# Pairs of keys apart, and VectorE squares for softmax sums and new rows

## The chip, the cores and the metric

The kernel runs on one core of a Trainium2 chip. The metric is the device time of one execution in microseconds (us). A core has TensorE (PE in the profile, its weight loads PEld), VectorE (DVE), ScalarE (ACT), GpSimd (POOL) and SyncE (SP), which here issues every transfer (DMA). Each engine works through its own queue in order.

## The reference

One layer of an encoder with two head groups, for a prompt of 1024 rows and a sample of 32 rows, all in float32:

- `hn = rmsnorm(h)`; `[qA kA vA gA qB kB vB gB] = hn @ w_in`, each 512 wide: 8 heads of 64.
- A: band attention. Scores `q k / 8` plus a position bias, softmax over a frame's own chunk of 64 and the 8 chunks before it.
- B: stick-breaking attention, strictly causal: weight = sigmoid(z) times the product of sigmoid(-z) over the keys between.
- `y = concat(oA * silu(gA), oB * silu(gB)) @ w_out`; `h = h + rmsnorm(y)`; `h = h + sigmoid(h @ w_ple_gate) * (p @ w_ple)`.

Outputs are the two results and the new keys and values of A and B, of the prompt (A: the last 512 rows; B: all) and of the sample (32 rows).

## The kernel before, in words

The 1056 rows (`T`: 1024 of the prompt, `SEQ`, and 32 of the sample) are normed and turned once, then projected in three chunks of 352 columns. A projected group `st` has features on partitions and rows in columns; columns 1024 to 1055 are the sample's. Heads are worked in pairs, A0 B0 A1 B1 A2 B2 A3 B3; while one pair's attention runs, the next pair's k, q, v are projected, and the gates `gA`, `gB` at the end (`weave` puts the two streams together). After that come the output product and the gate product.

Attention takes a head's queries in blocks of 128, i = 0 to 7. For each block there are three steps: scores (`scores`), turning of the weights, so that keys lie on partitions (`weights_t`), and, once per four blocks, the product with the values (`values`). In A a block has `cost(i)` = i + 1 key blocks, at most 5; in B i + 1. In `scores`, A takes score plus bias and the running extreme on VectorE (into `om`), then ScalarE makes the exponential (`om` to `be`) and its sum into a column of `sums`. In B ScalarE makes sigmoids, VectorE a running product (`TENSOR_TENSOR_SCAN`), and GpSimd a difference (`om` to `be`).

The weights are turned in one of two ways. Blocks 0 to 3 (and B's last, 7) go through TensorE: transposes into the PSUM banks with tag "T" (two of them; tiles `ptwA`, `ptwB`), from which ScalarE and VectorE take a rounded part `wTh` and the rest `wTl`. Blocks in `ROUND` (A: 4 to 7, B: 4 to 6) are turned by squares of 32 by 32 on VectorE (`STREAM_TRANSPOSE`, `om` from `be`), go out to a DRAM scratch (`swapA`, `swapB`) and come back with the four partition groups in place (`be` from `swapA`), and are then split into `wTh` and `wTl`. For this the four columns of a group of four keys have to lie apart, in four stretches. The view `apart` does it when the exponential or the difference is written:

```
return x.rearrange("p (b c k) -> p b k c" if out else "p (b k c) -> p b k c", c=4, k=32)
```

Consecutive elements are so written 32 columns (128 bytes) from one another, and the transpose reads its input in a row.

Three small things are also turned on TensorE, each by one transpose into a "T" bank and a ScalarE copy: A's softmax sums (`ptsA`, evicted to `sumrowA`, [8, 128], stored to `rs_dr`, from which the gates read them over partitions as `oggA`), the sample's 32 new rows of keys (`ptkA`, `ptkB`, in `short_block`, called by `keys_out`) and of values (`ptvA`, `ptvB`, by `values_out`). The sums are preceded by a reciprocal on VectorE. The long part of keys is turned by squares (`ktA`, `ktB`) and stored by quarters of partitions. The long part of values is turned by squares that read every second column (`vxA`, `vxB`), goes through a scratch and back into `st`, and is copied to `vtA`, `vtB`, from which `prep_v` makes `v2A`, `v2B`. The new rows of values are stored twice, to the output and to the scratch `vs_dr`, from which the sample's attention loads them. The tiles `kt`, `vx`, `vt` share the tag "tok" (two buffers).

Nothing is issued in the order in which it is written. A recorder notes every operation with what it depends on; a planner with fixed prices per operation (`cost`) plays the program through, gives each operation off TensorE a due time (`due`), and fixes every engine's order (`plan`), four times over. TensorE's priorities are the order of recording. The price of a transpose on VectorE is 100 + 1.04 ns per column, or another for a view with four axes. All instructions stand under line 497 in the profile, where the recorder emits them; they are told apart by the names of their tiles.

Of the kernel before, what the change touches and what calls it, by code (L numbers as in the profile page):

```python
# [8 lines left out]
F32 = mybir.dt.float32  # L9
# [4 lines left out]
P = 128  # L14
D = 1024
SEQ = 1024
NS = 32
T = SEQ + NS
# [484 lines left out]
def stream_step(  # L503
# [20 lines left out]
        return Buf(shape, F32, name=name, real=dram.tile(shape, F32, tag=name, name=name))  # L524

    o_dr = [scratch([P, T], f"o_dr{n}") for n in range(8)]
    rs_dr = scratch([8, T], "rs_dr")
    og_dr = scratch([8, P, T], "og_dr")
    h1_dr = scratch([T, D], "h1_dr")
    sum_dr = {w: scratch([4, 4, P, 512], f"sum_dr{w}") for w in "og"}  # L530
# [41 lines left out]


    NAMES = ["qA", "kA", "vA", "gA", "qB", "kB", "vB", "gB"]

    def fixed_columns():
        x = small.tile([8, NS], F32, tag="fixed", name="fixed")
        nc.gpsimd.memset(x, 1.0)
        dma(rs_dr[:, SEQ:T], x)

    raws, loaded = {}, {}

# [48 lines left out]

    def scale_x(t, xt, n, gp):
        sq = ring1.tile([P, D], f"sq{t}")
        ms = small.tile([P, 1], F32, tag="ms", name=f"ms{t}", bufs=4)
        nc.scalar.activation(sq[0:n], xt[0:n], AF.Square, scale=1.0 / 32.0, accum_out=ms[0:n])
        r = rstd_of(ms, f"rs{t}", n)
        for kh in range(2):
            nc.vector.scalar_tensor_tensor(sq[0:n, HALF[kh]], xt[0:n, HALF[kh]], r[0:n], gp[kh][0:n], ALU.mult, ALU.mult)
        return sq
# [65 lines left out]
        return (0 if ab == "A" else 4) + p  # L705


    def short_block(src, out, nm):
        pt = psum("T", nm)
        nc.tensor.transpose(pt[0:NS, 0:P], src[:, SEQ:T], ident)  # L710
        nc.scalar.copy(out[0:NS, 8, :], pt[0:NS, 0:P])

    def keys_out(ab, p, src, o_p, o_s):

        n = SEQ // 2 if ab == "A" else SEQ
        h2 = slice(2 * p, 2 * p + 2)

        def turn():
            out = at2.tile([P, NT, P], F32, tag="tok", name=f"kt{ab}{p}", bufs=2)
            x = out.rearrange("p b c -> p (b c)")[:, 0:n]  # L720
            nc.vector.transpose(x, src()[:, SEQ - n:SEQ])
            rows = o_p[0, 0, :, h2, :].rearrange("(c t) h d -> t c (h d)", t=32)
            for g in range(4):
                q = slice(32 * g, 32 * g + 32)
                dma(rows[:, :, q], x[q].rearrange("t (c f) -> t c f", f=32))
            short_block(src(), out, f"ptk{ab}{p}")
            dma(o_s[0, 0, :, h2, :].rearrange("p h d -> p (h d)"), out[0:NS, 8, :])

        return [(0.1, turn)]

    def values_out(ab, p, src, o_p, o_s, then):

        h2 = slice(2 * p, 2 * p + 2)
        b0 = 4 if ab == "A" else 0
        box = {}

        def turn():
            st = src()
            D = scratch([2, 4, HD, SEQ // 4], f"swap{ab}{p}")
            x = at2.tile([P, SEQ], F32, tag="tok", name=f"vx{ab}{p}", bufs=2)  # L740
            nc.vector.transpose(x.rearrange("p (i j b f) -> p b i j f", i=2, j=2, f=32), st[:, 0:SEQ].rearrange("p (b i t j) -> p b i j t", i=2, t=32, j=2))
            dma(D.rearrange("i g (t j) x -> (g t) i (j x)", j=2), x.rearrange("p (i x) -> p i x", i=2))
            for i in range(2):
                dma(st[HD * i:HD * i + HD, 0:SEQ].rearrange("p (g x) -> p g x", g=4), D[i].rearrange("g p x -> p g x"))
            out = at2.tile([P, NT, P], F32, tag="tok", name=f"vt{ab}{p}", bufs=2)
            box["out"] = out
            short_block(st, out, f"ptv{ab}{p}")

        def back():
            out = box["out"]  # L750
            nc.scalar.copy(out[:, 0:8, :].rearrange("p b (g f) -> p g b f", g=4), src()[:, 0:SEQ].rearrange("p (g b f) -> p g b f", g=4, f=32))
            dma(o_p[0, 0, :, h2, :].rearrange("(b p) h d -> p b (h d)", p=P), out[:, b0:8, :])
            dma(o_s[0, 0, :, h2, :].rearrange("p h d -> p (h d)"), out[0:NS, 8, :])
            then(out)

        return [(0.1, turn), (0.0, back)]
# [7 lines left out]
    def col_steps(j):  # L764
# [56 lines left out]

        def after_v(tok):
            src_of["v", ab, p] = tok
            dma(vs_dr[ab][:, p * P:(p + 1) * P], tok[0:NS, 8, :])

        if k == "q":
            steps.append((0.0, after_q))
# [8 lines left out]
    def attention(ab, p, h):  # L836
# [5 lines left out]
        def begin():  # L842
            if ab == "A":
                bias = at2.tile([P, 640], F32, tag="bias", name=f"bias{nm}", bufs=2)
                dma(bias, bias_src(2 * p + h, P, 0, 640))
                nc.gpsimd.memset(bias[0:HD, 0:HD], -NEG)
                nc.gpsimd.memset(bias[HD:P, 576:640], -NEG)
                box["bias"] = bias
                box["sums"] = small.tile([P, 8], F32, tag="sums", name=f"sums{nm}", bufs=2)

        def lo_block(i):
            return max(0, i - 4) if ab == "A" else 0
# [19 lines left out]
        def apart(i, x, out=False):  # L872

            if i not in together:
                return x
            return x.rearrange("p (b c k) -> p b k c" if out else "p (b k c) -> p b k c", c=4, k=32)

        def scores(i):
            L, kd, kl = Lq[h], KDh[h], KLD[h]
            b0 = lo_block(i)  # L880
            n = (i + 1 - b0) * P
            k0 = b0 * P
            cut = [0, n] if n <= 512 else [0, n // 2, n]
            w0, w1 = rooms(i)
            pieces = []
            for j in range(len(cut) - 1):
                s = psum("S", f"S{nm}_{i}_{j}")[:, 0:cut[j + 1] - cut[j]]
                lhs = L[:, i * P:(i + 1) * P]
                ks = slice(k0 + cut[j], k0 + cut[j + 1])
                nc.tensor.matmul(s, lhs, kd[:, ks], start=True, stop=False)  # L890
                nc.tensor.matmul(s, lhs, kl[:, ks], start=False, stop=True)
                pieces.append((cut[j], cut[j + 1], s))
            if ab == "B":
                a, b, s = pieces[-1]
                dg = s[:, b - a - P:b - a]
                nc.vector.tensor_tensor(dg, dg, maskb, ALU.add)
                nc.gpsimd.memset(w0[:, n:n + 1], 1.0)
                for a, b, s in pieces:
                    nc.scalar.activation(w0[:, a:b], s, AF.Sigmoid, scale=-1.0)
                for a, b, s in reversed(pieces):  # L900
                    rev = w0[:, a:b][:, ::-1]
                    nc.vector.tensor_tensor_scan(rev, rev, s, w0[:, b:b + 1], ALU.mult, ALU.bypass)
                nc.gpsimd.tensor_tensor(apart(i, w1[:, 0:n], True), apart(i, w0[:, 1:n + 1]), apart(i, w0[:, 0:n]), ALU.subtract)
            else:
                m = small.tile([P, 4], F32, tag="stat", name=f"stat{nm}_{i}", bufs=6)
                sums = box["sums"]
                for j, (a, b, s) in enumerate(pieces):
                    nc.vector.tensor_tensor_reduce(
                        w0[:, a:b], s, box["bias"][:, n - b:n - a][:, ::-1], 1.0,
                        3e38 if j == 0 else m[:, j - 1:j], ALU.add, ALU.min, m[:, j:j + 1])  # L910
                last = len(pieces) - 1
                nc.scalar.activation(apart(i, w1[:, 0:n], True), apart(i, w0[:, 0:n]), AF.Exp, bias=m[:, last:last + 1], scale=-1.0, accum_out=sums[:, i:i + 1])
                if i == 7:
                    nc.vector.reciprocal(sums, sums)
                    pt = psum("T", f"pts{nm}")
                    nc.tensor.transpose(pt[0:8, 0:P], sums, ident)
                    row = at.tile([P, 4 * P], F32, tag="ot", name=f"sumrow{nm}", bufs=2)[0:8, 0:P]
                    nc.scalar.copy(row, pt[0:8, 0:P])
                    dma(rs_dr[2 * p + h, 0:SEQ].rearrange("(i q) -> i q", q=P), row)
            state[i] = w0, w1  # L920

        wT = {}
# [5 lines left out]
        def weights_t(i):  # L928
# [9 lines left out]
            if i in together:  # L938
# [5 lines left out]
                w0, w1 = whole[group]  # L944
                m = sum(cost(x) for x in group)
                first = {x: sum(cost(y) for y in group[:k]) for k, x in enumerate(group)}
                squares = w0[:, 0:m * P].rearrange("p (c b q) -> p b c q", c=4, q=32)
                for x, _, _ in done_with:
                    y = slice(first[x], first[x] + cost(x))
                    nc.vector.transpose(squares[:, y], w1[:, y.start * P:y.stop * P])  # L950
                dr = scratch([4, P, m * 32], f"swap{nm}_{i}")
                dma(dr.rearrange("g (k c) x -> (g k) (c x)", c=4), w0[:, 0:m * P])
                dma(w1.rearrange("p (g x) -> p g x", g=4), dr.rearrange("g p x -> p g x"))
# [493 lines left out]
        dma(*x)  # L1447
        rec.behind()
    bias_rows()
    fixed_columns()  # L1450
    for h in range(4):
        dma(masks[h * NS:(h + 1) * NS, :], maskb[0:NS, 0:NS])
    for j in range(3):
# [176 lines left out]
    class Row:  # L1630


        def __init__(self, t, h1):
            self.t, self.h1 = t, h1
            self.t0, self.n = rows_of(t)
            self.ms = small.tile([P, 2], F32, tag="ms2", name=f"ms2_{t}", bufs=4)

        def load(self):
            self.x = [wpool.tile([P, 512], F32, tag="wr", name=f"x2_{self.t}_{q}", bufs=4) for q in range(2)]
# [277 lines left out]
```

## Time and profile before

| | |
|---|---|
| median of 3 runs | 797.52 us (795.85 to 797.86) |
| the profiled execution, its own time | 796.99 us |
| span in the profile | 795.2 us |
| mean granted TensorE clock | 0.997 |
| busy: PE, DVE, ACT, POOL | 772.9, 600.3, 519.7, 447.9 us |
| moved by DMA | 177.83 MB, 224 GB/s |

The span goes from the first to the last instruction. In a row of a group stand the engine, the operation, output and input by their names in the program, the shape and the count; then the busy time, the mean in ns of one, and the engine's idle time just before them with what ended it. In a list of waits a row gives the waiting engine and tile, what it waited for, the total in us, how often, and the longest. A window's row gives its limits and length, then busy time and instructions of PE, PEld, DVE, ACT and POOL, the granted clock, the DMA engines' share, and GB/s. A timeline's row begins with the start and the duration in us. A row of transfers ends with the size of one and the median us from issue to landing. Matmuls overlap in TensorE's pipeline, and their ends are modelled.

### The profile page before, as it was taken

How to read it: one execution, taken by the hardware profiler on the slowest of the kernel's cores; microseconds unless marked ns; L12 is line 12 of the kernel's file. 1: busy time of each engine (PE TensorE's matmuls, PEld its weight loads, DVE VectorE, ACT ScalarE, POOL GpSimd, SP SyncE). 2: the span in 40 equal slices, each digit the busy share in tenths (PEclk: the TensorE clock that was granted, in tenths of full speed). 3: DMA queues.
4: the chain of work that ended last, by engine and by line, in shares of the span. 5: the costliest groups of instructions: out<-in, count | busy, mean ns of one | idle time of the engine just before them, and what ended most of it. 6: DMA issues, size and time to landing. Idle time of an engine off the chain costs nothing. (4 is left out here: it accounts for less than half of the span.)

```text
span 795.2 us, 13848 instructions
## 1 busy us (share of the span) xinstructions
PE 772.9 (97%) x4518; PEld 709.4 (89%) x4518; DVE 600.3 (75%) x1007; ACT 519.7 (65%) x1039; POOL 447.9 (56%) x503
## 2 busy tenths in 40 slices
PE   8999999999999999999999999999999999999997
PEld 6999989998999999889999888999997877888786
DVE  6716788897889985799899788985446878686655
ACT  5636686577696644896567786542349867876741
POOL 5624638883556876234652327788634358597613
PEclk9999999999999999999999999999999999999999
DMA  8519998778988869776557668884769857569734
GB/s 268 164 45 288 247 280 284 236 222 295 252 261 261 261 196 258 213 214 204 136 161 169 204 203 259 255 241 142 229 228 336 276 172 269 202 228 314 230 110 133
DMA packets 176330, 177.83 MB, mean 224 GB/s; under 512 B 38129, under 2 KB 132057, under 8 KB 176258
## 3 DMA queue, kind: packets, MB, share of 16 engines
q1 hardware_dynamic: 176258, 176.95, 73.6%
q8 instruction: 36, 0.59, 0.3%
q14 instruction: 36, 0.29, 0.1%
HBM read 107.62 MB, written 60.88 MB: 212 GB/s over the span
## 5 line engine op out<-in xcount | busy, mean ns | idle before, releaser
L497 POOL TENSOR_TENSOR be<-om 128x128 f32<-128x128 f32 (+7 forms) x64 | 84.0, 1324 | 57.2 <-DVE om L497 10.5
L497 DVE TENSOR_TENSOR_SCAN om<-om,SB 128x384 f32<-128x384 f32 (+5 forms) x96 | 94.3, 999 | 9.9 <-ACT om L497 5.0
L497 ACT ACTIVATE be<-om,statA 128x640 f32<-128x640 f32 (+4 forms) x64 | 63.9, 1021 | 9.6 <-DVE wTl L497 4.2
L497 DVE TENSOR_TENSOR wTl<-be,wTh 128x640 fp32r<-128x640 f32 (+2 forms) x56 | 62.2, 1115 | 10.6 <-ACT wTh L497 10.4
L497 DVE STREAM_TRANSPOSE om<-be 128x640 f32<-128x640 f32 (+2 forms) x56 | 49.6, 888 | 11.4 <-ACT be L497 8.0
L497 ACT ACTIVATE om<-SB 128x384 f32<-128x384 f32 (+5 forms) x96 | 44.7, 491 | 20.2 <-DVE SB L497 9.8
L497 ACT CAST wTh<-be 128x640 fp32r<-128x640 f32 (+2 forms) x56 | 43.3, 774 | 12.7 <-DMA be<-swapB 7.0
L497 POOL TENSOR_TENSOR oB<-oB,oB 128x256 f32<-128x256 f32 x32 | 26.8, 862 | 15.0 <-DMA oB<-in_w_out_dram 14.8
L497 DVE CUSTOM_DVE_ANT_0 om<-SA,biasA 128x320 f32<-128x320 f32 (+2 forms) x64 | 29.7, 482 | 7.0 <-PE SA L497 5.2
L497 POOL TENSOR_TENSOR gB<-gB,gB 128x256 f32<-128x256 f32 x32 | 28.3, 902 | 11.9 <-DMA gB<-in_w_ple_gate_dram 10.8
L497 POOL TENSOR_TENSOR klB<-stkB,kdB 64x1024 fp32r<-64x1024 f32 x8 | 19.4, 2426 | 26.7 <-ACT kdB L497 25.6
L497 PE MATMUL SB<-kdB,LB 128*128 128x384 f32 (+5 forms) x96 | 33.5, 351 | 0.7 <-DVE om L497 0.7
L497 ACT CAST wTh<-ptwB 128x512 fp32r<-128x512 f32 (+3 forms) x48 | 22.2, 482 | 17.7 <-PE ptwB L497 15.8
L497 PE MATMUL SB<-klB,LB 128*128 128x384 f32 (+5 forms) x96 | 32.9, 347 | 0.0
L497 PE MATMUL SA<-kdA,LA 128*128 128x320 f32 (+2 forms) x96 | 30.1, 323 | 0.9 <-DVE statA L497 0.7
L497 DVE TENSOR_TENSOR wTl<-ptwB,wTh 128x512 fp32r<-128x512 f32 (+3 forms) x48 | 25.2, 542 | 5.9 <-ACT wTh L497 4.5
L497 PE MATMUL SA<-klA,LA 128*128 128x320 f32 (+2 forms) x96 | 29.3, 317 | 0.2 <-DMA klA<-klA 0.2
L497 POOL TENSOR_TENSOR sggA<-sggA,oggA 128x352 f32<-128x352 f32 x24 | 25.7, 1075 | 6.4 <-DVE sggA L497 2.3
L497 POOL TENSOR_TENSOR klA<-stkA,kdA 64x1024 fp32r<-64x1024 f32 x8 | 20.9, 2608 | 6.9 <-ACT kdA L497 6.5
L497 PE MATMUL PVB<-wTh,v2B 128*128 128x512 f32 (+1 forms) x96 | 21.6, 349 | 2.8 <-DVE otA L497 1.9
L497 POOL TENSOR_TENSOR h<-h,x 128x512 f32<-128x512 f32 (+1 forms) x18 | 23.6, 1337 | 0.0
L497 POOL TENSOR_TENSOR sggB<-sggB,oggB 128x352 f32<-128x352 f32 x12 | 11.9, 988 | 20.3 <-DVE sggB L497 15.7
(707 smaller groups left out, 2630.7 us busy)
## 6 DMA issues: line engine op xcount, KB each, us to landing
swapA<-om SPq DMA_DIRECT2D x32, 320.0 KB, 4.3
be<-swapA SPq DMA_DIRECT2D x32, 320.0 KB, 4.8
oB<-in_w_out_dram SPq DMA_DIRECT2D x16, 256.0 KB, 5.2
sum_dro<-oB SPq DMA_DIRECT2D x16, 256.0 KB, 4.0
gB<-in_w_ple_gate_dram SPq DMA_DIRECT2D x16, 256.0 KB, 4.6
sum_drg<-gB SPq DMA_DIRECT2D x16, 256.0 KB, 4.7
x<-in_x_prompt_dram SPq DMA_DIRECT2D x16, 256.0 KB, 3.5
h_dr<-h SPq DMA_DIRECT2D x8, 512.0 KB, 3.9
```

What stands on the lines that cost most here:

```text
L497: getattr(getattr(tc.nc, o.what[0]), o.what[1])(*args, **kw)
```

## The change

- `apart`: of each four consecutive keys, the first two go to the first half of the block's columns and the other two to the second half, pair beside pair. Elements are so written in pairs of neighbours.
- `weights_t`: the squares read every second column of a half. Their output lies as before, and so do the transfers.
- `short_block` is gone. `keys_out` turns the sample's 32 columns in the same transpose as the long part; `values_out` does it with a transpose of its own into a wider `vx`. The new function `new_rows` stores them from 128 partitions in pieces of 32 elements, for values once to the output and once to `vs_dr`, both in `turn` (before, the row to the output was stored in `back`).
- A's sums: `sums` has 32 columns, the last 24 set to 1.0 by GpSimd at the start of a head; VectorE turns them by squares, and all 128 partitions are stored. `rs_dr` gets rows of 32 x 128; the ones that `fixed_columns` stored once for the sample's columns now come with them.
- Tags of small tiles (`ms`, `ms2`) are joined.

```diff
-    rs_dr = scratch([8, T], "rs_dr")
+    rs_dr = scratch([8, 32 * P], "rs_dr")
...
-    def fixed_columns():
-        x = small.tile([8, NS], F32, tag="fixed", name="fixed")
-        nc.gpsimd.memset(x, 1.0)
-        dma(rs_dr[:, SEQ:T], x)
...
-    def short_block(src, out, nm):
-        pt = psum("T", nm)
-        nc.tensor.transpose(pt[0:NS, 0:P], src[:, SEQ:T], ident)
-        nc.scalar.copy(out[0:NS, 8, :], pt[0:NS, 0:P])
+    def new_rows(x, dst):
+        dma(dst.rearrange("t (g f) -> g t f", f=32), x)
...
-            out = at2.tile([P, NT, P], F32, tag="tok", name=f"kt{ab}{p}", bufs=2)
-            x = out.rearrange("p b c -> p (b c)")[:, 0:n]
-            nc.vector.transpose(x, src()[:, SEQ - n:SEQ])
+            x = at2.tile([P, NT * P], F32, tag="tok", name=f"kt{ab}{p}", bufs=2)[:, 0:n + NS]
+            nc.vector.transpose(x, src()[:, SEQ - n:T])
...
-            short_block(src(), out, f"ptk{ab}{p}")
-            dma(o_s[0, 0, :, h2, :].rearrange("p h d -> p (h d)"), out[0:NS, 8, :])
+            new_rows(x[:, n:n + NS], o_s[0, 0, :, h2, :].rearrange("p h d -> p (h d)"))
...
-            x = at2.tile([P, SEQ], F32, tag="tok", name=f"vx{ab}{p}", bufs=2)
+            x = at2.tile([P, T], F32, tag="tok", name=f"vx{ab}{p}", bufs=2)
+            nc.vector.transpose(x[:, SEQ:T], st[:, SEQ:T])
+            new_rows(x[:, SEQ:T], o_s[0, 0, :, h2, :].rearrange("p h d -> p (h d)"))
+            new_rows(x[:, SEQ:T], vs_dr[ab][:, p * P:(p + 1) * P])
+            x = x[:, 0:SEQ]
...
-            short_block(st, out, f"ptv{ab}{p}")
...
-            dma(o_s[0, 0, :, h2, :].rearrange("p h d -> p (h d)"), out[0:NS, 8, :])
...
-            dma(vs_dr[ab][:, p * P:(p + 1) * P], tok[0:NS, 8, :])
...
-                box["sums"] = small.tile([P, 8], F32, tag="sums", name=f"sums{nm}", bufs=2)
+                box["sums"] = small.tile([P, 32], F32, tag="sums", name=f"sums{nm}", bufs=2)
+                nc.gpsimd.memset(box["sums"][:, 8:32], 1.0)
...
-            return x.rearrange("p (b c k) -> p b k c" if out else "p (b k c) -> p b k c", c=4, k=32)
+            return x.rearrange("p (c k d) -> p k c d" if out else "p (k c d) -> p k c d", c=2, d=2)
...
-                    nc.vector.reciprocal(sums, sums)
-                    pt = psum("T", f"pts{nm}")
-                    nc.tensor.transpose(pt[0:8, 0:P], sums, ident)
-                    row = at.tile([P, 4 * P], F32, tag="ot", name=f"sumrow{nm}", bufs=2)[0:8, 0:P]
-                    nc.scalar.copy(row, pt[0:8, 0:P])
-                    dma(rs_dr[2 * p + h, 0:SEQ].rearrange("(i q) -> i q", q=P), row)
+                    nc.vector.reciprocal(sums[:, 0:8], sums[:, 0:8])
+                    row = at.tile([P, 4 * P], F32, tag="ot", name=f"sumrow{nm}", bufs=2)[:, 0:32]
+                    nc.vector.transpose(row, sums)
+                    dma(rs_dr[2 * p + h].rearrange("(i g q) -> g i q", g=4, q=32), row)
...
-                squares = w0[:, 0:m * P].rearrange("p (c b q) -> p b c q", c=4, q=32)
+                squares = w0[:, 0:m * P].rearrange("p (i j b q) -> p i j b q", i=2, j=2, q=32)
...
-                    nc.vector.transpose(squares[:, y], w1[:, y.start * P:y.stop * P])
+                    nc.vector.transpose(squares[:, :, :, y], w1[:, y.start * P:y.stop * P].rearrange("p (i b k j) -> p i j b k", i=2, k=32, j=2))
```

More of the change, by code (lines that the diff above doesn't have):

```diff
@@ L633, in scale_x @@
         sq = ring1.tile([P, D], f"sq{t}")
-        ms = small.tile([P, 1], F32, tag="ms", name=f"ms{t}", bufs=4)
+        ms = small.tile([P, 2], F32, tag="ms", name=f"ms{t}", bufs=4)[:, 0:1]
         nc.scalar.activation(sq[0:n], xt[0:n], AF.Square, scale=1.0 / 32.0, accum_out=ms[0:n])
@@ L724, in turn @@
                 q = slice(32 * g, 32 * g + 32)
-                dma(rows[:, :, q], x[q].rearrange("t (c f) -> t c f", f=32))
-            short_block(src(), out, f"ptk{ab}{p}")
-            dma(o_s[0, 0, :, h2, :].rearrange("p h d -> p (h d)"), out[0:NS, 8, :])
+                dma(rows[:, :, q], x[q, 0:n].rearrange("t (c f) -> t c f", f=32))
+            new_rows(x[:, n:n + NS], o_s[0, 0, :, h2, :].rearrange("p h d -> p (h d)"))
         return [(0.1, turn)]
@@ L1449, in stream_step @@
     bias_rows()
-    fixed_columns()
     for h in range(4):
@@ L1635, in __init__ @@
             self.t0, self.n = rows_of(t)
-            self.ms = small.tile([P, 2], F32, tag="ms2", name=f"ms2_{t}", bufs=4)
+            self.ms = small.tile([P, 2], F32, tag="ms", name=f"ms2_{t}", bufs=4)
         def load(self):
```

## The prediction, made before the changed kernel was run

> **What bounds the kernel now.** I read the page first (busy shares), then a window over the attention stage, then what TensorE waits for, then the groups by shape.
>
> ```profile
> span 795.2 us, 13848 instructions
> PE 772.9 (97%) x4518; PEld 709.4 (89%) x4518; DVE 600.3 (75%) x1007; ACT 519.7 (65%) x1039; POOL 447.9 (56%) x503
> ```
> ```profile
> 60.00:500.00 440.00, 426.73 (x2689) 408.46 (x2688) 369.78 (x650) 311.62 (x618) 244.11 (x280) 1.00 0.81 232
> 380.00:440.00 60.00, 59.76 (x380) 57.70 (x379) 54.54 (x87) 41.69 (x80) 27.75 (x28) 1.00 0.60 162
> ```
>
> TensorE (PE) sets the time: 97% over the span. All that the change touches lies between 60 and 500 us, where the two attentions run beside the projections. There PE is busy 426.73 of 440 us, so 13.3 us of visible gaps are left, VectorE (the third busy figure) has 70.2 us free, ScalarE (the fourth) 128.4. No other engine is the bound; what can be won is a PE gap or PE work. In 380 to 440 VectorE has only 5.5 us free: it is the engine next in line.
>
> The gaps of PE, by what ended them:
>
> ```profile
> PE ptsA L497 <- DVE sumsA L497: 5.2, 7, 1.5
> PE PVB L497 <- DVE otA L497: 1.9, 1, 1.9
> PE ptkB L497 <- ACT stkB L497: 1.1, 1, 1.1
> PE PVB L497 <- ACT wTh L497: 0.9, 1, 0.9
> PE SA L497 <- DVE statA L497: 0.7, 2, 0.5
> PE SB L497 <- DVE om L497: 0.7, 2, 0.5
> PE PVA L497 <- ACT wTh L497: 0.6, 2, 0.3
> PE SsA L497 <- ACT QsA L497: 0.5, 1, 0.5
> PE ptwA L497 <- ACT sumrowA L497: 0.5, 1, 0.5
> PE ptosA L497 <- ACT be L497: 0.4, 1, 0.4
> PE ptvB L497 <- ACT stvB L497: 0.2, 1, 0.2
> ```
>
> The largest gap is a step that the change removes: PE stands still seven times for the reciprocal of A's softmax sums, to turn them (`ptsA`). The turning of new keys and values (`ptkB`, `ptvB`) and the eviction of the turned sums (`sumrowA`) add 1.1, 0.2 and 0.5. Together 7.0 us.
>
> **Part 1: the 24 small transposes leave PE.** Eight for sums, eight for new keys, eight for new values. Their own time:
>
> ```profile
> 83.96 0.27 PE L497 MATMUL ptkB<-ident,stkB 128*32 128x128 f32 x1
> 83.98 0.57 PE L497 MATMUL mm_qB<-hnh,wh_qB 128*128 128x352 f32 x2
> ```
> ```profile
> 731.08 0.87 PE pth L497 x8
> ```
>
> The matmul behind `ptkB` starts 0.02 us after it, although the row gives 0.27 for one (spans overlap in PE's pipeline); transposes in a row take 0.87/8 = 0.109 each. So 24 of them cost 0.5 us to 2.6 us; the first row is of the instruction itself, I take 0.5. With the waits, up to 7.5 us of PE. In the timeline of the first such wait, the instructions queued behind `ptsA` are score and projection matmuls, whose operands stand ready: they start at once, so what is behind the wait was held by it alone.
>
> What is late next? PE would come up to 1.5 us earlier per head to the products with the values (`PVA`), which wait for `wTh`, at the end of the chain exponential, transpose, out to DRAM and back, cast. That chain also gets shorter, by part 2: four exponentials a head. So I keep 6.0 of the 7.0, a choice, since some gaps will open elsewhere; were the exponentials not faster, half, 3.5.
>
> **Part 2: the exponential writes pairs.**
>
> ```profile
> L497 ACT ACTIVATE be<-om,statA 128x640 f32<-128x640 f32 x32 | 46.1, 1481 | 1.1 <-PE ptwA L497 1.1
> L497 ACT ACTIVATE be<-om,statA 128x512 f32<-128x512 f32 x8 | 5.8, 722 | 1.2 <-DVE wTl L497 1.1
> L497 ACT ACTIVATE be<-om,statA 128x384 f32<-128x384 f32 x8 | 4.9, 613 | 3.1 <-DVE wTl L497 3.1
> ```
> ```profile
> L497 DVE STREAM_TRANSPOSE om<-be 128x640 f32<-128x640 f32 x40 | 33.0, 829 | 8.9 <-ACT be L497 8.0 <-POOL be L497 0.8
> L497 DVE STREAM_TRANSPOSE om<-be 128x896 f32<-128x896 f32 x8 | 8.8, 1105 | 1.5 <-POOL be L497 1.2 <-POOL om L497 0.3
> L497 DVE STREAM_TRANSPOSE ktB<-stkB 128x1024 f32<-128x1024 f32 x4 | 5.0, 1238 | 2.5 <-ACT stkB L497 2.5
> L497 DVE STREAM_TRANSPOSE vxA<-stvA 128x1024 f32<-128x1024 f32 x4 | 4.9, 1234 | 0.7 <-ACT stvA L497 0.6
> ```
>
> Blocks 0 to 3 write in a row, 4 to 7 write each element 128 bytes from the last. The straight ones grow by 109 ns per 128 columns (613 to 722), so 640 in a row would be 831; the scattered one takes 1481. The excess is 650 ns, 1.02 per element. The trace has no ScalarE write in pairs. Its bounds: 1481 (nothing won), 831 (all won), and not above 1481, as the jumps are halved; if each jump kept its price, 831 + 325 = 1156. The nearest row is `vxA`: a transpose that reads every second column (`(b i t j)`, j = 2), thus also two elements of each four, at 1234 against 1238 for `ktB`, which reads in a row: free. I take 831: 32 x 0.65 = 20.8 us of ScalarE's time, between 0 and 20.8. With the 24 evictions that go,
>
> ```profile
> L497 ACT COPY sumrowA<-ptsA 8x128 f32<-8x128 f32 x8 | 2.0, 248 | 1.1 <-DMA o_dr<-otA 0.5 <-PE ptsA L497 0.4
> L497 ACT COPY ktA<-ptkA x4: 238/245/252, 63.9 to 381.5; 32x128 f32<-32x128 f32 x4
> ```
>
> 24 x 0.25 = 6.0 us, ScalarE loses 26.8 of its 311.6 us in the stage.
>
> [...] At 1156, the price by jumps, half of ScalarE's gain would be lost, and the sum would be 4.8 + 0.5 + 1.0 = 6.3 us in place of 8.5.
>
> ScalarE is not the bound, so its 26.8 us count only where somebody waits for it. VectorE does:
>
> ```profile
> DVE om L497 <- ACT be L497: 8.3, 15, 1.2
> DVE sumsA L497 <- ACT be L497: 4.2, 8, 0.7
> ```
>
> These 12.5 us, transposes and reciprocals behind exponentials, reach PE through the waits that the change does not remove: 1.9 + 0.9 + 0.7 + 0.7 + 0.6 + 0.5 + 0.4 = 5.7 us. The single 1.9 hangs on a transfer of values; of the other 3.8 I take half, 2.0 rounded up. Bounds: 0 and 5.7.
>
> **Part 3: transposes read every second column.** 56 of them (40 of 640 columns, 8 of 768, 8 of 896; 38,912 columns). By `vxA` they cost what they do now, and I take 0. The other end is ScalarE's price for a jump, 1.02 ns: 39.7 us more on VectorE. Below nothing: the output is contiguous runs of 32 as before, so a gain is excluded. The planner's price goes by the number of axes of the view, and neither the old nor the new view has the four that it asks for, so its due times for them stay.
>
> **Part 4: what VectorE takes over.** Eight transposes of 32 columns for sums, eight for values, 32 columns more for eight of keys. From 640 to 1024 columns the rows grow by (1238 - 829)/384 = 1.07 ns a column, leaving 829 - 682 = 147 fixed: 0.18 for 32 columns. 16 x 0.18 + 8 x 0.03 = 3.1 us.
>
> ```profile
> L497 DVE RECIPROCAL sumsA<-sumsA 128x8 f32<-128x8 f32 x8 | 1.6, 203 | 4.2 <-ACT be L497 4.2
> L497 POOL MEMSET om<- 128x1 f32 x66 | 5.6, 105 | 7.7 <-DMA swapA<-om 3.3 <-DMA swapB<-om 2.5 <-issue 1.5
> L497 POOL TENSOR_TENSOR be<-om 128x640 f32<-128x640 f32 x8 | 12.2, 1530 | 7.0 <-DVE om L497 3.1 <-ACT wTh L497 2.3 <-DVE wTl L497 1.6
> L497 POOL TENSOR_TENSOR be<-om 128x512 f32<-128x512 f32 x8 | 8.8, 1098 | 11.1 <-DVE wTl L497 5.3 <-issue 2.4 <-DVE om L497 2.1
> L497 POOL TENSOR_TENSOR be<-om 128x1024 f32<-128x1024 f32 x8 | 18.2, 2270 | 5.3 <-ACT QsB L497 1.5 <-DVE om L497 1.3 <-ACT QfsB L497 1.3
> ```
>
> Its bounds are 0.8 us (16 x 0.034 + 0.3, columns alone) and 3.5 (the short ones at the reciprocal's 203 ns). VectorE's 70.2 free us cover it, and the 12.5 us that it waits for exponentials shrink; without that cover it would be 3.1 us at most, so I count 0. GpSimd gets eight memsets of 24 columns (0.1 each, 0.8 us) and is idle for 44% of the stage: 0. Its subtraction for B also writes pairs now: a scattered 640 takes 1530, a straight one by its neighbours 1098 + 1172/4 = 1391, so at most 0.14 x 8 = 1.1 us off the path: 0.
>
> **Part 5: transfers.** The rows of new keys, values (output and scratch) and sums go out as 128 pieces of 128 bytes where they were 32 or 8 of 512; one transfer (`fixed`) goes, none is added.
>
> ```profile
> out_dram<-ktA SPq DMA_DIRECT2D x16, 64.0 KB, 3.2
> out_dram<-ktA SPq DMA_DIRECT2D x4, 16.0 KB, 4.6
> 123.14 0.34 SPq L497 DMA_DIRECT2D out_dram<-vtB  x1
> 124.04 0.46 SPq L497 DMA_DIRECT2D swapB<-vxB  x1
> 124.56 1.58 SPq L497 DMA_DIRECT2D vs_drB<-vtB  x1
> ```
>
> The first row is already of 128-byte pieces, four times as much, and lands in 3.2 us, not later than the second in 512-byte pieces. The values' row to the output moves from `back` to `turn`, in front of the swap on SP's queue, and the scratch row with it: at worst 2 x 0.46 us before a swap; but the scratch row already leaves within a microsecond of it. I take 0; the bound is 0.9 us for each of eight pairs, on the path only where the 1.9 us wait stands.
>
> **Sum.** 6.0 + 0.5 + 2.0 = 8.5 us. The profiled execution took 796.99 (span 795.2 and 1.8 around it): 788.5. The median of the runs shown, 797.52, is 0.5 above it, so 789.0. Best: the whole 13.3 us of gaps plus 2.6 of PE work, 15.9, gives 781.6. Worst of this case: exponentials as slow as now (3.5 + 0 + 0, half of it lost): a gain of 1.8, about no change.
>
> **The rivals.** First, the gain is taken back (no measurable change): the waits for `ptsA` are only the place where PE, ahead of its partners, meets them, and it then meets `wTh` and `statA` instead. For it: VectorE is 84% busy in the stage and its 5.5 free us in 380 to 440 leave little. Against it: PE's own list of waits is short, and the chain behind gets 2.6 us shorter a head (4 x 0.65), more than any `ptsA` wait. About 796.5.
>
> Second, reads of every second column are not free in this shape (slower): 39.7 us on VectorE, evenly 5.4 in a stretch of 60 us, all of what 380 to 440 has free. If half reached PE, 789 + 20 = 809. It decides against the change from 8.5 us through to PE, some 0.44 ns per column at that half. Against it: `vxA`.
>
> Third, the new list gives a new order (slower), since every engine's queue is planned afresh: one pair's values come back a transfer later, and `PVB` waits for them.
>
> ```profile
> 485.69 5.95 DMA stvB<-swapB
> ```
>
> Such a transfer is 5.95 us on the chain; two of them give 789 + 11.9 = 800.9, and from one and a half (8.5/5.95) the change loses. For it: the 1.9 us wait shows that one pair has no slack there. Against it: PE's priorities are the recorded order, which stays, and the scratch and output rows leave no later.
>
> **How the numbers follow.** The forecast, a gain of 2.5 to 16 us, 0.74; taken back, 0.12; slow reads, 0.04; late values, 0.10. A difference under 0.3% (2.4 us) can't be told from none here; so faster 0.74, same 0.12, slower 0.14. The range goes from the best sum, 781.5, to 798.0, which takes in the second case and leaves out the slow reads and most of the late values, some 0.13.
>
> **What would show it.** [...] The prediction is wrong if PE's gaps return under `PVA`, `PVB` or `SA`, or if VectorE's transposes grow.

## The result, and the profile after

The changed kernel takes 793.53 us (median, 792.28 to 795.34) against 797.69 beside it: a ratio of 0.9951 with a 95% interval of 0.9931 to 0.9970. It is faster by 4.2 us, where 8.5 were forecast; half of the gain is missing.

The page's first lines and three windows of the changed kernel (in a window: busy time and count of PE, PEld, DVE, ACT, POOL, then the granted clock), and behind them one window of the kernel before:

```profile
span 791.2 us, 13810 instructions
PE 769.2 (97%) x4494; PEld 708.2 (90%) x4494; DVE 599.9 (76%) x1023; ACT 507.2 (64%) x1019; POOL 443.9 (56%) x510
```
```profile
60.00:500.00 440.00, 428.86 (x2698) 412.76 (x2697) 374.08 (x674) 303.04 (x607) 245.07 (x290) 1.00 0.81 235
200.00:260.00 60.00, 55.15 (x343) 52.73 (x342) 49.75 (x90) 46.10 (x85) 34.41 (x48) 0.97 0.83 252
380.00:440.00 60.00, 60.00 (x383) 58.30 (x382) 51.60 (x91) 39.62 (x83) 23.45 (x27) 1.00 0.58 161
```
```profile
200.00:260.00 60.00, 59.09 (x379) 56.59 (x379) 52.45 (x95) 44.58 (x88) 37.78 (x49) 1.00 0.89 261
```

In 60 to 500 us PE has 11.1 us of gaps (13.3 before), and 4.9 of them stand in 200 to 260 (0.9 before), where the clock is below 1 as well. The costs of the parts, by shape, and last the row of table loads of the kernel before:

```profile
L497 ACT ACTIVATE be<-om,statA 128x640 f32<-128x640 f32 x32 | 28.6, 898 | 2.0 <-DVE statA L497 1.2 <-DVE wTl L497 0.7
L497 ACT ACT_TABLE_LOAD x16 | 20.5, 1283 | 2.2 <-DMA swapA<-om 1.1 <-PEq L1895 0.7 <-DVE SB L497 0.2
L497 DVE STREAM_TRANSPOSE om<-be 128x640 f32<-128x640 f32 x40 | 33.0, 832 | 3.8 <-ACT be L497 3.5
L497 DVE STREAM_TRANSPOSE sumrowA<-sumsA 128x32 f32<-128x32 f32 x8 | 1.6, 206 | 0.6 <-DMA o_dr<-otB 0.4
L497 DVE STREAM_TRANSPOSE vxA<-stvA 128x32 f32<-128x32 f32 x4 | 0.8, 198 | 0.0
```
```profile
L497 ACT ACT_TABLE_LOAD x12 | 15.4, 1283 | 0.9 <-PEq L1905 0.7
```

The exponential went from 1481 to 898 ns, the transposes stayed (829 to 832). What PE waits for now (the largest rows, without two at the start of the span):

```profile
PE SB L497 <- DVE om L497: 3.9, 3, 3.2
PE PVB L497 <- ACT wTh L497: 2.0, 1, 2.0
PE SA L497 <- DVE statA L497: 1.7, 2, 0.9
PE ptksB L497 <- DMA be<-in_cache_b_k_dram: 1.6, 1, 1.6
PE mm_kA L497 <- ACT wh_kA L497: 1.2, 1, 1.2
```

The waits for sums and new rows are gone, all 7.0 us; others took their place, the longest 3.2 us from 228.9 to 232.1 us. (The wait of `PVB` for `wTh` lies at 509 us, behind the stage.) Around the longest, ScalarE goes to and fro between exponentials (A1) and sigmoids (B1), loading a table each time. A piece of its timeline (start, duration), and the matmul that ends the gap:

```profile
224.79 1.28 ACT L497 ACT_TABLE_LOAD   x1
226.09 0.39 ACT L497 ACTIVATE om<-SB 128x256 f32<-128x256 f32 x1
226.49 0.44 ACT L497 COPY be<-PVsA 32x64 f32<-32x64 f32 x2
226.95 1.28 ACT L497 ACT_TABLE_LOAD   x1
228.24 0.88 ACT L497 ACTIVATE be<-om,statA 128x640 f32<-128x640 f32 x1
229.02 0.18 ACT L497 ACTIVATION_READ_ACCUMULATOR be<-om,statA 128x1 f32 x1
229.22 1.28 ACT L497 ACT_TABLE_LOAD   x1
```
```profile
232.10 0.42 PE L497 MATMUL SB<-kdB,LB 128*128 128x320 f32 x1 [3.21 <-DVE om L497]
```

16 loads in all, where the kernel before had 12.

### The profile page after: what moved, and what is told of

The parts are those of the page before. It is cut to its first block, busy times and chain, and to the rows that moved or that the text cites. A ratio compares the mean times of both kernels' runs of the same rounds, so it can differ in the third digit from the quotient of the medians.

```text
span 791.2 us, 13810 instructions
## 1 busy us (share of the span) xinstructions
PE 769.2 (97%) x4494; PEld 708.2 (90%) x4494; DVE 599.9 (76%) x1023; ACT 507.2 (64%) x1019; POOL 443.9 (56%) x510
## 4 chain that ended last, share of the span: by engine, by line
PE 80%; DMA 7%; DVE 3%; ACT 3%; issue 2%; SPq 2%; POOL 2%; DVEq 0%; ACTq 0%; POOLq 0%
PE mm_gB L497 6%; PE mm_qA L497 6%; PE mm_vA L497 6%; PE mm_kA L497 6%; PE mm_kB L497 4%; PE mm_qB L497 4%; PE mm_vB L497 4%; PE PVB L497 4%; PE mm_gA L497 4%; PE SB L497 4%; PE PVA L497 3%; PE g0P L497 2%; PE SA L497 2%; PE o0P L497 2%; PE g2P L497 2%; PE o1P L497 2%
## 5 line engine op out<-in xcount | busy, mean ns | idle before, releaser
L497 POOL TENSOR_TENSOR be<-om 128x896 f32<-128x896 f32 (+7 forms) x64 | 80.0, 1257 | 42.2 <-DVE om L497 10.1
L497 ACT ACTIVATE be<-om,statA 128x640 f32<-128x640 f32 (+4 forms) x64 | 46.4, 728 | 11.9 <-DVE wTl L497 6.1
L497 DVE CUSTOM_DVE_ANT_0 om<-SA,biasA 128x320 f32<-128x320 f32 (+3 forms) x64 | 29.9, 483 | 14.6 <-PE SA L497 7.3
L497 POOL TENSOR_TENSOR gB<-gB,gB 128x256 f32<-128x256 f32 x32 | 26.2, 840 | 9.1 <-DMA gB<-in_w_ple_gate_dram 6.5
L497 DVE TENSOR_TENSOR SB<-SB,maskb 128x128 f32<-128x128 f32 x64 | 17.6, 289 | 8.4 <-PE SB L497 8.0
L497 POOL TENSOR_TENSOR sggB<-sggB,oggB 128x352 f32<-128x352 f32 x12 | 12.2, 1019 | 20.3 <-DVE sggB L497 11.5
L497 PEld LDWEIGHTS SB<-kdB,LB 128*128 128x128 f32 x96 | 18.1, 189 | 5.8 <-DVE om L497 5.4
```

What stands on the lines that cost most here:

```text
L497: getattr(getattr(tc.nc, o.what[0]), o.what[1])(*args, **kw)
```

## The experiments

Three questions: what is each part worth; is the missing gain taken back because PE meets other waits (the first rival); or is it the new order (the third), and if so, the table loads in it?

**Pairs alone.** The prices of the planner are the same for the old and new views, so this kernel has, instruction by instruction, the order of the kernel before.

```diff
-            return x.rearrange("p (b c k) -> p b k c" if out else "p (b k c) -> p b k c", c=4, k=32)
+            return x.rearrange("p (c k d) -> p k c d" if out else "p (k c d) -> p k c d", c=2, d=2)
...
-                    nc.vector.transpose(squares[:, y], w1[:, y.start * P:y.stop * P])
+                    nc.vector.transpose(squares[:, :, :, y], w1[...].rearrange("p (i b k j) -> p i j b k", i=2, k=32, j=2))
```

> The kernel before with the pairs and the squares of every second column alone; every engine's order is that of before, instruction by instruction. Theory (the parts are worth what was priced, the new order costs some 4 us): the exponentials alone bring the 2.5 + 2.0 us that the prediction hung on them, about 793 us. Rival (the gain is taken back because TensorE meets other waits): under 1 us, about 797. Both expect 898 ns for the exponential of 640.

Measured: 787.81 us against 797.19, ratio 0.9878 (0.9857 to 0.9899): 9.4 us, more than the whole change brings. PE's waits in this kernel:

```profile
PE PVB L497 <- DVE otA L497: 2.2, 1, 2.2
PE idle L497 <- DVE newh L497: 1.3, 1, 1.3
PE ptp L497 <- DMA pp<-in_p_prompt_dram: 1.1, 1, 1.1
PE SA L497 <- DMA klA<-klA: 0.9, 1, 0.9
PE ptwA L497 <- ACT sumrowA L497: 0.9, 1, 0.9
PE PVB L497 <- ACT wTh L497: 0.6, 1, 0.6
PE SsA L497 <- ACT QsA L497: 0.5, 1, 0.5
```

The eight transposes of sums still run on PE here, but nothing waits for their reciprocals any more: those had been late because the exponentials were. The pairs also shorten GpSimd's subtraction in this order (1530 to 1384 ns), a part that this run doesn't separate.

**The moves alone, in the changed kernel's order.** Same views restored in the changed kernel; its order and its 16 table loads stay.

> The changed kernel with the exponentials written as before, element by element; every engine's order is that of the changed kernel, its 16 table loads too. Theory: 3.5 + 0.5 us gained by the transposes that leave TensorE, 4 lost by the order: about 797.5 us, no change. Rival: the order costs nothing, the transposes alone bring the whole 4 us: about 793.5.

Measured: 801.25 us, ratio 1.0047 (1.0027 to 1.0067): 4.1 us slower than before. So pairs are worth 7.7 us in this order too (801.25 to 793.53), and it is moves and order together that lose.

**Fewer table loads.** In the changed kernel and in the one before, the first sigmoids of a pair of B are made to depend on the last exponentials of the pair of A; 8 loads remain of 16 and of 12. `exps[p]` holds the exponentials of pair p of A as recorded.

```diff
                     nc.scalar.activation(w0[:, a:b], s, AF.Sigmoid, scale=-1.0)
+                    if h == 0:
+                        rec.ops[-1].after.update(exps[p])
```

> The changed kernel, with the first sigmoids of a pair of B made to come after the last exponentials of the pair of A (an added dependency; 8 table loads in place of 16). Theory: the 4 us between the forecast and the result come back, about 789 us, and the gap of 3.2 us at 228 us is gone. Rival: TensorE meets other waits, about 793.

> The kernel before with the same added dependency (8 table loads in place of 12). Theory: the price of alternation is the alternation's, not the change's: four loads of 1.28 us fewer bring some 2 us here too, about 795.5. Rival: no change, 797.5.

Measured: 793.05 us, ratio 0.9953 (0.9931 to 0.9975), and 797.19 us, ratio 1.0004 (0.9981 to 1.0026). No gain in either: the missing 4 us didn't come back with the loads, and the theory fell. The gap at 228 us is gone from the changed kernel, but its waits are now

```profile
PE SA L497 <- DVE statA L497: 2.9, 4, 1.0
PE PVB L497 <- ACT wTh L497: 1.7, 1, 1.7
PE SB L497 <- DVE om L497: 1.4, 2, 1.1
```

The dependency changed the plan everywhere, and gaps opened in other places. This test therefore can't say what eight loads cost by themselves.

**All moves, in the order of the kernel before.** The program is planned as it was; when it is emitted, a moved operation stands in the place of the one that it replaces (the transposes on PE are left out, a transpose on VectorE is issued where the copy on ScalarE stood, transfers go out in their old turn in pieces of 128 bytes, and GpSimd's ones are written behind the first exponential of a head). Values' new rows are turned into the tile `vt`, since `vx` is free by then. The core of it:

```diff
+                if o.instead is not None:
+                    o.instead(tc.nc)
+                    continue
...
                     nc.tensor.transpose(pt[0:8, 0:P], sums, ident)
+                    rec.instead(lambda _: None)
...
                     nc.scalar.copy(row, pt[0:8, 0:P])
+                    rec.instead(lambda real: real.vector.transpose(whole_row[:, 0:32].get(), sums.get()))
```

> Pairs and all the moves (sums, new keys, new values turned by VectorE, stored in pieces of 128 bytes), but every engine keeps the order of the kernel before: the moved operations stand where the replaced ones stood, so the planner had no say. Theory (the order costs, the moves don't): under the 787.8 us of the run with pairs alone, about 785 to 788. Rival (the moves cost by themselves, by VectorE's extra work or the small pieces on the queue): about 793, as the changed kernel.

Measured: 785.01 us against 796.51, ratio 0.9859 (0.9834 to 0.9883): 11.5 us faster than before, the fastest kernel of the study. The operations are those of the changed kernel, but for 12 table loads in place of 16, which come from the order; where they stand differs. The traces bear the order out: but for what was moved or left out, every engine's list is that of the kernel before. The page's first lines, the window and the waits:

```profile
span 782.3 us, 13779 instructions
PE 769.8 (98%) x4494; PEld 708.5 (91%) x4494; DVE 599.0 (77%) x1023; ACT 501.2 (64%) x1015; POOL 446.9 (57%) x510
```
```profile
60.00:500.00 440.00, 436.37 (x2755) 420.40 (x2754) 378.90 (x680) 300.45 (x610) 253.83 (x300) 1.00 0.83 240
```
```profile
PE SA L503 <- DVE statA L503: 1.4, 2, 1.2
PE idle L503 <- DVE newh L503: 1.3, 1, 1.3
PE ptp L503 <- DMA pp<-in_p_prompt_dram: 1.2, 1, 1.2
PE PVB L503 <- DVE wTl L503: 0.8, 1, 0.8
PE SA L503 <- DMA klA<-klA: 0.7, 2, 0.5
```

PE is busy for 436.4 of the 440 us, against 428.9 in the changed kernel: 7.5 us fewer gaps, and 57 more matmuls done by 500 us. The ratios differ by 0.9%, 7 us, with some 2.5 us either way by their intervals. VectorE's extra work and the small pieces cost nothing that shows on net: the kernel isn't slower than pairs alone (0.9859 and 0.9878, closer than their intervals).

**The moves alone, in the order of the kernel before.**

> The moves (sums, new keys and values to VectorE) without the pairs, every engine in the order of the kernel before. Theory (both parts end the same waits, so that their gains overlap): 4 us or so for the moves alone, about 792.5, though they add only 2.8 us to the pairs. Rival (gains add): 2.8 us, about 793.7, and the waits of TensorE for the sums reappear elsewhere.

Measured: 791.60 us against 798.27, ratio 0.9931 (0.9903 to 0.9958): 6.7 us. With the pairs' 9.4 that would be 16.1; both together bring 11.5. So 4.6 us, with some 3 either way by the intervals, are won by either part alone. The waits for sums, 5.2 us before, fit this: pairs end them, and so do the moves.

**Other orders of the same operations.** One price of the planner is altered by 100 ns; nothing else. It is the time that a transfer takes to land (2600 in place of 2500) or, in one run, the time from a landed transfer to the engine that waits for it ("wake", 300 in place of 200). The edit for the landing:

```diff
-DMA_RATE, LANDING, WAKE_DMA = 320.0, 2500, 200
+DMA_RATE, LANDING, WAKE_DMA = 320.0, 2600, 200
```

> The changed kernel with one price of the planner altered (a transfer lands after 2600 ns in place of 2500): the same operations, another order; 14 table loads. Theory (the order is a draw): some us away from 793.5, to either side, 786 to 800. Rival (the moves cost): 793.5 within 1.

> The changed kernel with another price altered (300 ns in place of 200 from a landed transfer to the engine that waits): a third order of the same operations. Theory (a draw): another time again, 786 to 800. Rival (the moves cost): 793.5 within 1.

> The kernel with pairs alone and the same altered price. Theory (a draw): some us away from 787.8, more likely slower, 786 to 798. Rival (only the moves cost): 788 within 1.

> The kernel before with the planner's landing price at 2600 in place of 2500: the order that the run with pairs alone had at that price, with the exponentials of before. Theory (the order of the kernel before is a lucky one): 6 us or so above the kernel before, about 803. Rival (the order matters only once the exponentials are fast): 797.

| operations | order | table loads | median us | ratio to before (95%) |
|---|---|---|---|---|
| before | its own | 12 | 797.19 | 1 |
| before | landing 2600 | 12 | 804.55 | 1.0085 (1.0057 to 1.0113) |
| pairs alone | before's | 12 | 787.81 | 0.9878 (0.9857 to 0.9899) |
| pairs alone | landing 2600 | 12 | 794.16 | 0.9970 (0.9951 to 0.9988) |
| moves alone | before's | 12 | 791.60 | 0.9931 (0.9903 to 0.9958) |
| moves alone | changed kernel's | 16 | 801.25 | 1.0047 (1.0027 to 1.0067) |
| changed kernel | its own | 16 | 793.53 | 0.9951 (0.9931 to 0.9970) |
| changed kernel | landing 2600 | 14 | 796.28 | 0.9996 (0.9974 to 1.0019) |
| changed kernel | wake 300 | 14 | 790.01 | 0.9927 (0.9904 to 0.9950) |
| changed kernel's | before's | 12 | 785.01 | 0.9859 (0.9834 to 0.9883) |

Each ratio is to the kernel before as it ran beside that row (medians of 796.51 to 798.27), so rows are best compared by ratio. The changed kernel's operations take 785.0 to 796.3 us in four orders: 11 us without any change of work but table loads. Its own order and wake 300 can't be told apart by their intervals; the other two can. With single elements the same two orders, before's and the changed kernel's, lie 9 us apart (0.9931 and 1.0047).

The number of table loads doesn't explain this: with 14 loads each, two orders of the changed kernel are 6 us apart, with 12 each the two of the kernel before and the two of pairs alone are 7 apart, and the run with 8 loads above is no faster than the one with 16.

For each of the four sets of operations the order of the kernel before is the best one tried, of two, two, two and four. Whether that is luck, or whether the planner's prices had been fitted to that kernel, no run shows; a new list or price gave it up each time. The differences that pairs make within one order agree within some 2 to 3 us: 9.4 us in before's, 9 at a landing of 2600 (1.0085 to 0.9970), 7.7 in the changed kernel's.

**Writing in a row, reading every fourth column.** The pairs kernel's order, but the exponential and GpSimd's difference write straight, and the square reads with a step of 16 bytes. Against that kernel:

```diff
-            return x.rearrange("p (c k d) -> p k c d" if out else "p (k c d) -> p k c d", c=2, d=2)
+            return x
...
-  ... .rearrange("p (i b k j) -> p i j b k", i=2, k=32, j=2) ...
+  ... .rearrange("p (b k i j) -> p i j b k", i=2, k=32, j=2) ...
```

> The kernel before with its order, but exponential and difference written in a row and the squares read every fourth column, 16 bytes apart. Theory (what costs is a new stretch of 16 bytes for each element, whichever side it is on): exponential of 640 near 831 ns, transpose of 640 from 829 to about 1300 to 1480; VectorE loses some 20 us and the time is 798 to 806. Rival (only writes pay): transposes at 829 and the time at or under 787.8.

```profile
L497 DVE STREAM_TRANSPOSE om<-be 128x640 f32<-128x640 f32 x40 | 52.7, 1328 | 0.9 <-ACT be L497 0.3 <-POOL be L497 0.2
L497 ACT ACTIVATE be<-om,statA 128x640 f32<-128x640 f32 x32 | 26.4, 828 | 1.5 <-PE ptwA L497 1.1 <-DVE Vl2sA L497 0.3
```

Measured: 798.36 us, ratio 1.0008 (0.9987 to 1.0030). The exponential is at 828, the transpose at 1328. What ScalarE wins VectorE loses (its busy time is 621.5 us, 600.3 before), and with it the 9 us. A read with a step of 16 bytes from element to element is dear: 1328 ns, against 832 in the changed kernel, where the step is 8 bytes. So is a write of single elements 128 bytes apart: 1481, against 898 for pairs. For the write, pairs leave 70 ns (898 against 828) of the 653 (1481 against 828) standing. So the price shows on both sides, at the steps that were run; no run has a write with a step of 16 bytes.

## Why the prediction was wrong

The direction was right; the size was not, 4.2 us for 8.5, and the step that failed is one that the sum doesn't contain: the price of the new order, put at nothing. Point by point:

- **Part 2, the exponential.** The duration was nearly right: 831 predicted, 898 measured, by the row `vxA` and not by half the jumps (1156). The effect was too low: 2.5 + 2.0 = 4.5 us were hung on it, and it brings 9.4 in the same order. Late exponentials fed more of PE's waits than the 5.7 us that were allowed for: those for sums most of all, which stood under part 1. ScalarE's busy time fell by 12.5 us over the span (519.7 to 507.2), not by 27; four more table loads took 5.1 of it back, and the rest is not traced.
- **Part 1, transposes off PE.** The 7.0 us of waits did go. But the share "kept" was put too high beside fast exponentials (6.0 + 0.5; the moves add 11.5 - 9.4 = 2.1 us to the pairs, which the intervals don't tell from none) and too low without them (3.5 + 0.5; measured 6.7). The sum lets fast exponentials raise what the moves are worth; in the old order they lower it, since both parts end the same waits.
- **Parts 3, 4 and 5, costs taken as nothing.** Right: transposes 832, short ones 0.2 us, VectorE's total 599.9 for 600.3, and no net loss with the small pieces in the old order.
- **The sum.** 8.5 us predicted for the parts; 11.5 measured in the old order. By itself this would have been an error to the low side, and two wrong terms in it partly cancel: part 2 was too low, part 1 beside it too high.
- **The new order.** This is the step that failed. The third rival named it, gave it 0.10, and set it down to a late transfer of values; no wait of PE in the changed kernel names such a transfer. Its counter-argument was that PE's priorities stay. They do, but the order in which PE's matmuls come out does not: lined up by name, some 1200 of the 4494 stand elsewhere in the changed kernel than in the run with the old order, and the other engines' queues are new as well. The price of the order is the 7 us between the same operations in two orders; a sum for a change that alters the list of operations needs a term for it, at least as a width.
- **The first rival** looks right in the changed kernel's waits (`statA` and `wTh` are there), but as the cause of the missing gain it is refuted: with the same operations in the old order PE's gaps over the span are 12.5 us (782.3 less 769.8) against 22.0 (791.2 less 769.2), although 1.4 of the 1.7 us for `statA` stay.

What in the new order costs the 7 us is settled only in part. In the profiled executions it is gaps of PE: the spans differ by 8.9 us, the gaps by 9.5, and PE's busy time by 0.6 the other way. It is not the number of table loads alone, as the table of orders shows. A share can be the clock. The next two rows are windows of the changed kernel, the one around the long gap and the one behind it:

```profile
220.00:240.00 20.00, 15.63 (x91) 14.64 (x90) 13.54 (x29) 19.25 (x31) 8.70 (x18) 0.91 0.87 276
233.40:236.60 3.20, 2.78 (x9) 2.78 (x10) 2.93 (x5) 3.15 (x7) 2.63 (x4) 0.50 0.75 248
```

After the gap, and one of 1.2 us right behind it, PE runs at half clock (granted 0.50; matmuls of `mm_kA` start 0.30 us apart, and 0.16 apart behind it), here over 3.2 us, which can cost 1.6 us of work (an estimate, half of it). Over the timed executions the mean granted clock was 0.992 to 0.997 in the changed kernel and 0.997 to 1.000 with the old order, about 0.0045 apart in the middle: an estimate of at most 0.0045 x 791 = 3.6 us, if PE was never waiting meanwhile. How the 7 us divide between gaps and clock is not measured, and which single dependency makes the old order better stays open.

## What to carry to other kernels

Where a planner orders the queues, cost a change in two parts: its operations in the old order, and the new order, which here was a draw of lots over 11 us and, from an order that was already a good one, a loss in each case tried. To test an idea, hold the order fixed, as by putting the new operation where the old one stood; to ship it, the same trick kept all 11.5 us where planning anew kept 4.2. And when an engine waits for the end of a chain, the step that makes the chain late and the step at its end can be in part one gain, here about 4.6 of 16.1 us, and not two.

## What the runs showed of the hardware

- ScalarE writing float32 in pairs, each pair far from the last: 898 ns for 640 columns; one at a time, 128 bytes apart, 1481; in a row, 828.
- VectorE's transpose of 640 columns: 829 ns reading in a row, 832 every second column, 1328 every fourth.
- GpSimd's subtraction of 640 columns in the old order: 1387 ns with pairs, 1530 with single elements, 1383 in a row (the prediction's figure for that was 1391). The figure holds within one order only: in the changed kernel's order pairs take 1533, single elements 1684. With pairs in the old order:

```profile
L503 POOL TENSOR_TENSOR be<-om 128x640 f32<-128x640 f32 x8 | 11.1, 1387 | 7.0 <-DVE om L503 5.4 <-DVE wTl L503 1.6
```

- Behind one gap of PE of about 2 us the granted clock was 0.50 for a stretch, behind another it was 1.00. In the kernel before, PE waits 1.9 us for `otA` (the prediction's list of waits), until 496.2 us, and the window behind it reads:

```profile
496.30:499.70 3.40, 3.40 (x14) 3.21 (x15) 2.99 (x5) 0.78 (x3) 2.25 (x2) 0.50 1.02 249
```

In the changed kernel PE waits 2.0 us for `wTh` (the row `PVB`), until 510.7 us, and the window behind it is at full clock:

```profile
510.70:514.10 3.40, 3.40 (x20) 3.18 (x21) 1.29 (x3) 1.32 (x4) 0.04 (x1) 1.00 0.29 85
```

So the wait of 1.9 us was followed by 3.4 us at 0.50, and the wait of 2.0 us by 3.4 us at 1.00; what tells the two apart no run here shows.
